# Off-diagonal and state's part of a scan step first, diagonal part behind them, sums of squares with 64 columns of ones

## The chip, the cores and the metric

The kernel runs on one core of a Trainium2 chip. The core has five engines that run on their own and wait for one another by semaphores: TensorE (matmuls; PE in the profile, PEld for the loads of its stationary operand), VectorE (DVE), ScalarE (ACT), GpSimd (POOL) and SyncE (SP), which here issues transfers. The time of a run is the device time of the core in microseconds (us). Lower is better. Each engine works through its own instructions in the order in which the program wrote them.

## The reference

Two layers on an input of 1024 tokens by 1024 features, float32. The first is a chunked spatial-gating MLP, the second a Mamba-2 mixer, then a final RMSNorm. The change lies in the second layer's scan, which has 8 groups of 4 heads (64 features a head, 128 states) and 8 chunks of 128 tokens:

```
cb    = einsum('bclgn,bcsgn->bclsg', Cm, Bm)
w_ls  = cb[..., None] * decay * dt
y_diag = einsum('bclsgj,bcsgjp->bclgjp', w_ls, x)
states = einsum('bclgn,bclgj,bclgjp->bcgjpn', Bm, decay_to_end * dt, x)
prev   = scan over chunks: carry * chunk_decay + states
y_off  = einsum('bclgn,bcgjpn,bclgj->bclgjp', Cm, prev, exp(dA_cs))
y      = y_diag + y_off + x * d_skip
gated  = rmsnorm over each group's 256 features of (y * silu(z))
h      = h + gated @ w_out
```

## The kernel before, in words

The first 1010 us hold the first layer and most of the second layer's input projection. Then comes the scan, in an order written out by hand: `scans()` walks over n = 0 to 63, with group g = n // 8 and chunk c = n % 8. Between the scan's own small matmuls TensorE is given full-size matmuls, so that it has work while the other engines prepare the next step. Up to n = 50 these are the rest of the input projection (tile `ab`, helper `mm3`, L134 to L136), behind it the first product of the output projection (tile `bo`, the same lines).

Step n does, in this order of the program:

- `pe_b(n)` on TensorE: the **diagonal part**, four matmuls, one for each head, which each give 64 of the 128 rows of tile `yy` (L1626: 64 columns of the array, so heads 0 and 2 go to the lower, 1 and 3 to the upper half); for c > 0 the **off-diagonal part**, two full-width matmuls whose stationary operand is the state after chunk c - 1 (L1630); for c < 7 the **state's part**, one full-width matmul with 256 moving columns into tile `sp` (L1637). At c = 3 and c = 7 `pe_b` gets a group as `ends` and adds that group's **sums of squares** (`sum_b`, L1702): squares `gsq`, summed over the partitions by a matmul with ones as stationary operand, two matmuls for two halves of 256 tokens, into rows 0 and 64 of the right half of `sp`. For the last group they are four, as the squares' two halves are not added up before. ScalarE copies rows 0 and 64 out (L1706).
- some projection matmuls; `pe_a(n + 2)`: three transposes and a matmul into tile `tp` (L1593, L1594).
- `weights(n + 1)` on VectorE: the weights `wl` of the next diagonal part (L1617), behind ScalarE's `decay` (L1599, L1601).
- `update(n)` on VectorE: the state after chunk c, from `sp` and the carried state (L1656; L1654 at c = 0). It stands directly behind `weights(n + 1)`.
- `out(n)`: VectorE reads `yy`, the off-diagonal half first (L1668), then the diagonal half twice (L1671).
- `drain()`: a step of the convolution on a finished projection tile (L1322 on VectorE, L1328 on ScalarE); its last one frees the tile `ab`.
- `tokens(n + 2)`: VectorE (L1607, L1609), ScalarE (L1611) and GpSimd (L1612) make the operands of step n + 2 from `tp`; `gate(n)` on GpSimd; at some steps squares, stores and loads; more projection matmuls.

Diagonal and off-diagonal parts write the two halves of one PSUM tile `yy`; `yy`, `sp` and `tp` rotate through four buffers. After the scan the output projection runs alone, with one more `sum_b` (tile `pr`, four matmuls) inside it.

Every fp32 matmul of L1593 to L1702 appears in the profile as two instructions (four heads are 8 rows x8, two sums x4), each with its own weight load.

Of the kernel before, what the change touches and what calls it, by code (L numbers as in the profile page):

```python
# [15 lines left out]
P = 128  # L16
# [13 lines left out]
def kernel(  # L30
# [21 lines left out]
    nc = tc.nc  # L52
    x = x[0]
    out = out[0]
# [42 lines left out]
    def sm(name):  # L97
        return ps[0].tile([P, 512], F32, name=name, tag="sm", bufs=n_sm[0])
# [65 lines left out]
    ones = cst.tile([P, P], F32, name="ones")  # L164
# [1399 lines left out]
    class Scan:  # L1564
# [55 lines left out]
        def pe_b(self, c, ends=None):  # L1620

            w, wl = self.cw[c], self.wl.pop(c)
            yy = sm("yy")
            for j in range(4):
                pt, f = j // 2, j % 2
                nc.tensor.matmul(out=yy[f * 64:(f + 1) * 64, pt * P:(pt + 1) * P], lhsT=w[:, j * 64:(j + 1) * 64],  # L1626
                                 rhs=wl[:, j, :], start=True, stop=True)
            if c > 0:
                for pt in range(2):
                    nc.tensor.matmul(out=yy[:, 256 + pt * P:384 + pt * P],  # L1630
                                     lhsT=self.state[c - 1][:, pt * P:(pt + 1) * P], rhs=self.x(3, c),
                                     start=True, stop=True)
            sp = None
            if c < 7 or ends is not None:
                sp = sm("sp")
            if c < 7:
                nc.tensor.matmul(out=sp[:, 0:256], lhsT=w[:, 512:640], rhs=w[:, 256:512], start=True, stop=True)  # L1637
            if ends is not None:
                ends.sum_b(sp[:, 256:512], 2 if ends.g == G - 1 else 1)
            self.ps[c] = yy, sp  # L1640
# [57 lines left out]
        def sum_b(self, pr=None, n=1):  # L1698
            pr = sm("pr") if pr is None else pr
            for m in range(n):  # L1700
                for h in range(2):
                    nc.tensor.matmul(out=pr[h * 64:h * 64 + 1, 0:256], lhsT=ones[:, 0:1],  # L1702
                                     rhs=self.sq[:, m, h * 256:(h + 1) * 256], start=m == 0, stop=m == n - 1)
            self.sr = self.sq[:, 1, 0:256]
            for h in range(2):
                nc.scalar.copy(out=self.sr[h * 64:h * 64 + 1], in_=pr[h * 64:h * 64 + 1, 0:256])  # L1706
# [314 lines left out]
```

## Time and profile before

| what | value |
|---|---|
| median of the 3 runs shown | 1517.45 us (1517.34 to 1518.26) |
| the profiled execution | 1520.45 us, its span 1518.6 us |
| TensorE matmuls | 1475.8 us busy (97%), 7834 instructions |
| VectorE | 1052.2 us (69%) |
| ScalarE | 783.3 us (52%) |
| GpSimd | 402.8 us (27%) |
| DMA | 254.45 MB, mean 168 GB/s |
| scan, from the first diagonal matmul to the last | 1021.7 to 1356 us |

A row of the view in order of time gives the start in us from the span's start, the time from the first start to the last end of what was merged in it, the engine, the line, the operation, the tiles (out<-in), the shapes, and in brackets the idle time ahead and what ended it. Ends of matmuls are modelled, and one matmul begins before the one ahead has ended, so that starts are compared with starts. "issue" is idle time for which the profile names no other engine. A busy share of 97% does not say that TensorE streams all that time: a matmul that lasts longer because its weights were not there counts as busy.

### The profile page before, as it was taken

To read this page: it belongs to the slowest core of one execution; us is meant where nothing else is said; L and a number is where in the kernel's file an instruction comes from. 1 tells how busy PE (TensorE), PEld (TensorE's weight loads), DVE (VectorE), ACT (ScalarE), POOL (GpSimd) and SP (SyncE) were. 2 spreads that over 40 slices of the span, in tenths; PEclk is the share of its full clock that TensorE was granted. 3 is DMA by queue.
4 is the path that set the end of the run, shared out by engine and by line. 5 is a ranking of instruction groups with operands and counts; after the bars stand their busy time and mean duration, and the time that the engine had idled before them with its cause. 6 is when DMAs were issued, how large, how long until landed. Compare 5 with 4: busy or idle time off the path is not lost. (4 is left out here: it accounts for less than half of the span.)

```text
span 1518.6 us, 21307 instructions
## 1 busy us (share of the span) xinstructions
PE 1475.8 (97%) x7834; PEld 1219.9 (80%) x7834; DVE 1052.2 (69%) x1713; ACT 783.3 (52%) x1256; POOL 402.8 (27%) x451
## 2 busy tenths in 40 slices
PE   6899999999999999999999999989999999999997
PEld 6899988888888888877878788877777777777875
DVE  7956566676666655678656467867677777688876
ACT  6433332322322445556566556656676666756463
POOL 1111110000000023202131323117677666643121
PEclk9999999999999999999999999999999999999999
DMA  5554323332322999947377978787656564679973
GB/s 183 140 173 140 105 89 111 108 107 98 116 86 79 357 255 241 250 140 159 104 178 159 189 162 165 149 231 203 187 165 170 160 191 137 171 248 277 257 149 111
DMA packets 174952, 254.45 MB, mean 168 GB/s; under 512 B 16400, under 2 KB 103168, under 8 KB 171648
## 3 DMA queue, kind: packets, MB, share of 16 engines
q1 hardware_dynamic: 124768, 168.93, 36.6%
q0 software_dynamic: 42448, 70.27, 23.0%
q10 hardware_dynamic: 7632, 13.90, 2.6%
q8 instruction: 62, 1.02, 0.3%
q14 instruction: 42, 0.34, 0.1%
HBM read 186.14 MB, written 51.18 MB: 156 GB/s over the span
## 5 line engine op out<-in xcount | busy, mean ns | idle before, releaser
L134 PE MATMUL acc<-hh,wh 128*128 128x512 f32 x868 | 339.9, 392 | 1.7 <-ACT u L296 1.4
L136 PE MATMUL acc<-hh,wl 128*128 128x512 f32 x868 | 338.5, 390 | 2.0 <-DVE wl L112 1.8
L135 PE MATMUL acc<-hl,wh 128*128 128x512 f32 x868 | 337.8, 389 | 0.0
L112 DVE TENSOR_TENSOR wl<-wr,wh 128x1024 fp32r<-128x1024 f32 (+1 forms) x96 | 114.3, 1192 | 119.4 <-ACT wh L111 119.3
L136 PEld LDWEIGHTS acc<-hh,wl 128*128 128x128 f32 x868 | 162.9, 188 | 37.8 <-DVE wl L112 3.7
L134 PEld LDWEIGHTS acc<-hh,wh 128*128 128x128 f32 x868 | 163.1, 188 | 36.1 <-ACT u L296 2.3
L135 PEld LDWEIGHTS acc<-hl,wh 128*128 128x128 f32 x868 | 163.0, 188 | 33.1
L296 ACT COPY u<-acc 128x512 f32<-128x512 f32 x115 | 66.9, 583 | 197.7 <-PE acc L136 197.6
L111 ACT CAST wh<-wr 128x1024 fp32r<-128x1024 f32 (+1 forms) x112 | 115.2, 1029 | 95.4 <-PE acc L135 56.7
L136 PE MATMUL acc<-wh,hl 128*128 128x256 f32 x448 | 128.6, 287 | 4.8 <-DVE hl L407 3.4
L134 PE MATMUL acc<-wh,hh 128*128 128x256 f32 x448 | 129.2, 288 | 3.0 <-ACT hh L398 1.1
L134 PE MATMUL ab<-hh,wh 128*128 128x512 f32 x288 | 128.2, 445 | 2.8 <-DVE zt L999 1.7
L135 PE MATMUL acc<-wl,hh 128*128 128x256 f32 x448 | 128.1, 286 | 1.1 <-DVE wl L421 1.1
L136 PE MATMUL ab<-hh,wl 128*128 128x512 f32 x288 | 113.4, 394 | 0.0
L135 PE MATMUL ab<-hl,wh 128*128 128x512 f32 x288 | 112.5, 390 | 0.1
L136 PEld LDWEIGHTS acc<-wh,hl 128*128 128x128 f32 x448 | 87.1, 194 | 5.9 <-DVE hl L407 4.1
L134 PEld LDWEIGHTS acc<-wh,hh 128*128 128x128 f32 x448 | 87.3, 195 | 3.9 <-ACT hh L398 1.3
L135 PEld LDWEIGHTS acc<-wl,hh 128*128 128x128 f32 x448 | 87.2, 195 | 1.6 <-DVE wl L421 1.4
L1599 ACT ACTIVATE wl<-wl,tk 128x128 f32<-128x128 f32 x256 | 81.6, 391 | 2.2 <-DMA wl<-cs_d 1.9
L649 POOL DMA_DIRECT2D y_d<-y x8 | 4.4, 549 | 291.3 <-DVE y L646 291.3
L135 PE MATMUL bo<-wl,xh 128*128 128x512 f32 x192 | 76.2, 397 | 3.5 <-DVE wl L742 1.8
L112 DVE TENSOR_TENSOR wl<-t,wh 128x1024 fp32r<-128x1024 f32 (+1 forms) x38 | 45.5, 1196 | 48.5 <-ACT wh L111 48.4
(317 smaller groups left out, 3255.1 us busy)
## 6 DMA issues: line engine op xcount, KB each, us to landing
wr<-in_a_w_in_dram SPq DMA_DIRECT2D x48, 512.0 KB, 3.7
wl<-cs_d SPq DMA_DIRECT2D x64, 256.0 KB, 3.4
wr<-in_b_w_in_dram SPq DMA_DIRECT2D x30, 512.0 KB, 9.1
wb<-in_a_w_out_dram SPq DMA_DIRECT2D x10, 1024.0 KB, 11.8
wb<-in_b_w_out_dram SPq DMA_DIRECT2D x10, 1024.0 KB, 11.1
wr<-in_b_w_in_dram SPq DMA_DIRECT2D x36, 256.0 KB, 8.0
v<-v_d SPq DMA_DIRECT2D x8, 1024.0 KB, 4.8
y_d<-y POOLq DMA_DIRECT2D x8, 1024.0 KB, 5.8
```

Source lines behind the costliest of these rows:

```text
L111: nc.scalar.copy(out=hi, in_=src)
L112: return (eng or nc.vector).tensor_tensor(out=lo, in0=src, in1=hi.bitcast(F32), op=ALU.subtract)
L134: nc.tensor.matmul(out=o, lhsT=l[0], rhs=r[0], start=start, stop=False, **kw)
L135: nc.tensor.matmul(out=o, lhsT=l[0], rhs=r[1], start=False, stop=False, **kw)
L136: nc.tensor.matmul(out=o, lhsT=l[1], rhs=r[0], start=False, stop=stop, **kw)
L296: nc.scalar.copy(out=self.u[n][:, i], in_=a)
L649: store = lambda: nc.gpsimd.dma_start(out=y_d[-1], in_=y)
L1599: nc.scalar.activation(wl[:, j, :], wl[:, j, :], AF.Relu, scale=-1.0, bias=tokc(2, c, self.g)[:, j:j + 1])
```

## The change

In `pe_b` the four diagonal matmuls move from the front to behind the state's part; the sums of squares stay last. In `sum_b` the stationary operand is 64 columns of ones instead of one, so that each sum is written to 64 rows of PSUM in place of one; ScalarE still reads one row of each half. Nothing else differs: the instructions of VectorE, ScalarE, GpSimd and SyncE stand in the same order with the same operands.

```
@@ pe_b
             w, wl = self.cw[c], self.wl.pop(c)
             yy = sm("yy")
-            for j in range(4):
-                pt, f = j // 2, j % 2
-                nc.tensor.matmul(out=yy[f * 64:(f + 1) * 64, pt * P:(pt + 1) * P], lhsT=w[:, j * 64:(j + 1) * 64],
-                                 rhs=wl[:, j, :], start=True, stop=True)
             if c > 0:
                 for pt in range(2):
                     nc.tensor.matmul(out=yy[:, 256 + pt * P:384 + pt * P],
...
             if c < 7:
                 nc.tensor.matmul(out=sp[:, 0:256], lhsT=w[:, 512:640], rhs=w[:, 256:512], start=True, stop=True)
+            for j in range(4):
+                pt, f = j // 2, j % 2
+                nc.tensor.matmul(out=yy[f * 64:(f + 1) * 64, pt * P:(pt + 1) * P], lhsT=w[:, j * 64:(j + 1) * 64],
+                                 rhs=wl[:, j, :], start=True, stop=True)
             if ends is not None:
                 ends.sum_b(sp[:, 256:512], 2 if ends.g == G - 1 else 1)
             self.ps[c] = yy, sp
@@ sum_b
-                    nc.tensor.matmul(out=pr[h * 64:h * 64 + 1, 0:256], lhsT=ones[:, 0:1],
+                    nc.tensor.matmul(out=pr[h * 64:h * 64 + 64, 0:256], lhsT=ones[:, 0:64],
                                      rhs=self.sq[:, m, h * 256:(h + 1) * 256], start=m == 0, stop=m == n - 1)
```

On TensorE, at the step n = 11 (c = 3 of the second group), the rows around `pe_b`, those of before with a minus and those of the change with a plus (`yy<-wl,cw` is the diagonal part, `yy<-xbc,state` the off-diagonal, `sp<-cw` the state's part, `sp<-gsq,ones` the sums):

```order
 L135 MATMUL ab<-hl,wh 128x512
 L136 MATMUL ab<-hh,wl 128x512
-L1626 MATMUL yy<-wl,cw 64x128 x4
-L1630 MATMUL yy<-xbc,state 128x128 x2
-L1637 MATMUL sp<-cw 128x256
-L1702 MATMUL sp<-gsq,ones 1x256 x2
+L1626 MATMUL yy<-xbc,state 128x128 x2
+L1633 MATMUL sp<-cw 128x256
+L1636 MATMUL yy<-wl,cw 64x128 x4
+L1702 MATMUL sp<-gsq,ones 64x256 x2
 L134 MATMUL ab<-hh,wh 128x512
 L135 MATMUL ab<-hl,wh 128x512
```

The diagonal's four matmuls, 64 rows of output each, now stand next to the sums, which have 64 rows too; the two full-width parts stand next to the projection.

On TensorE, at the first step, n = 0, which has no off-diagonal part:

```order
 L1593 MATMUL tp<-ident,xbc 128x128 x3
 L1594 MATMUL tp<-xbc 128x128
-L1626 MATMUL yy<-wl,cw 64x128 x4
-L1637 MATMUL sp<-cw 128x256
+L1633 MATMUL sp<-cw 128x256
+L1636 MATMUL yy<-wl,cw 64x128 x4
 L134 MATMUL ab<-hh,wh 128x512
 L135 MATMUL ab<-hl,wh 128x512
```

The state's part, which needs the operands of `tokens`, has changed places with the diagonal part, which needs `wl`.

On VectorE nothing moves; the rows of one step that the prediction speaks of (c = 2 of the second group, `t` is what L1668 makes of the off-diagonal half) stand so before and with the change:

```order
L1617 TENSOR_TENSOR wl<-wl,cw 128x512
L1656 TENSOR_TENSOR state<-sp,state 128x256
L1668 TENSOR_TENSOR t_8700<-yy,ze 128x256
L1671 SCALAR_TENSOR_TENSOR cw<-xbc,dsk,yy 128x128 x2
L1322 SCALAR_TENSOR_TENSOR bc<-ab,par,bc 128x1021
```

The weights of the next diagonal part are made directly ahead of the state that the next off-diagonal part loads.

More of the change, by code (lines that the diff above doesn't have):

```diff
@@ L1623, in pe_b @@
             yy = sm("yy")
[L1624 to L1627, printed above, removed]
             if c > 0:
@@ L1637, in pe_b @@
                 nc.tensor.matmul(out=sp[:, 0:256], lhsT=w[:, 512:640], rhs=w[:, 256:512], start=True, stop=True)
+            for j in range(4):
+                pt, f = j // 2, j % 2
+                nc.tensor.matmul(out=yy[f * 64:(f + 1) * 64, pt * P:(pt + 1) * P], lhsT=w[:, j * 64:(j + 1) * 64],
+                                 rhs=wl[:, j, :], start=True, stop=True)
             if ends is not None:
@@ L1701, in sum_b @@
                 for h in range(2):
-                    nc.tensor.matmul(out=pr[h * 64:h * 64 + 1, 0:256], lhsT=ones[:, 0:1],
+                    nc.tensor.matmul(out=pr[h * 64:h * 64 + 64, 0:256], lhsT=ones[:, 0:64],
                                      rhs=self.sq[:, m, h * 256:(h + 1) * 256], start=m == 0, stop=m == n - 1)
```

## The prediction

> **What bounds the kernel now.** I read the page's head first, then the waits of TensorE from 1010 us on, then the order in time of TensorE in two single steps of the scan, and last the places where TensorE stands still. The head:
>
> ```profile
> span 1518.6 us, 21307 instructions
> ...
> PE 1475.8 (97%) x7834; PEld 1219.9 (80%) x7834; DVE 1052.2 (69%) x1713; ACT 783.3 (52%) x1256; POOL 402.8 (27%) x451
> ```
>
> TensorE is the bound nearly everywhere, and VectorE (DVE), the next, has a third of its time free. The 64 steps of the scan, which are all that the diff touches, start between 1020.7 and 1355.2 us, with projection matmuls between them. In the waits of the weight loads (columns: who waited for what; us in all, times, longest) no data is named for most of the idle time before the scan's own matmuls:
>
> ```profile
> PEld yy L1626 <- issue: 15.0, 42, 0.4
> PEld yy L1630 <- issue: 7.7, 45, 0.2
> ```
>
> That is some 0.35 us ahead of each diagonal part and 0.17 us behind it, where the profile knows of no semaphore. What it is shows in the order in time (start, us, engine, line). A step without sums of squares, n = 25:
>
> ```profile
> 1155.29 0.39 PE L136 MATMUL ab<-hh,wl 128*128 128x512 f32 x1
> 1155.61 0.66 PE L1626 MATMUL yy<-wl,cw 128*64 128x128 f32 x8
> 1156.20 0.71 PE L1630 MATMUL yy<-xbc,state 128*128 128x128 f32 x4
> 1156.74 0.60 PE L1637 MATMUL sp<-cw 128*128 128x256 f32 x2
> 1156.99 0.58 PE L134 MATMUL ab<-hh,wh 128*128 128x512 f32 x1
> 1157.41 0.39 PE L135 MATMUL ab<-hl,wh 128*128 128x512 f32 x1
> ```
>
> And n = 27, with them (the last of these rows is of the weight loads):
>
> ```profile
> 1165.26 0.39 PE L136 MATMUL ab<-hh,wl 128*128 128x512 f32 x1
> 1165.58 0.66 PE L1626 MATMUL yy<-wl,cw 128*64 128x128 f32 x8
> 1166.16 0.71 PE L1630 MATMUL yy<-xbc,state 128*128 128x128 f32 x4
> 1166.71 0.60 PE L1637 MATMUL sp<-cw 128*128 128x256 f32 x2
> 1167.24 0.60 PE L1702 MATMUL sp<-gsq,ones 128*1 128x256 f32 x4
> 1167.77 0.50 PE L134 MATMUL ab<-hh,wh 128*128 128x512 f32 x1
> 1168.10 0.39 PE L135 MATMUL ab<-hl,wh 128*128 128x512 f32 x1
> 1165.57 0.42 PEld L1626 LDWEIGHTS yy<-wl,cw 128*64 128x64 f32 x8 [0.35 <-ACT wl L1601]
> ```
>
> The durations of single instructions (ns, min/median/max) come from the lines' own rows:
>
> ```profile
> L1626 PEld LDWEIGHTS yy<-wl,cw x512: 132/137/137, 1021.7 to 1355.9; 128*64 128x64 f32 x171
> L1630 PE MATMUL yy<-xbc,state x112: 275/275/377, 1026.9 to 1277.1; 128*128 128x128 f32 x112
> L1702 PEld LDWEIGHTS sp<-gsq,ones x64: 79/82/84, 1058.8 to 1357.3; 128*1 128x1 f32 x64
> L1702 PE MATMUL sp<-gsq,ones x64: 377/377/379, 1058.8 to 1357.5; 128*1 128x256 f32 x64
> ```
>
> Matmuls overlap, so I count from start to start. A projection matmul takes 0.23 us (L134 and L135 end at 1157.57 and 1157.80; the rest of its 0.39 overlaps the next). The two of sp last 0.60 together, and one of 256 columns 0.38 alone (L1702), so 256 columns stream in 0.22 us. The diagonal's eight run in pairs side by side (64 columns of the array each): 0.66 less 0.27 over three and a half steps, 0.11 us a pair, 0.44 in all. The off-diagonal's four take 0.11 each, 0.44.
>
> From 1155.29 to 1157.41 are 2.12 us. The two projection matmuls account for 0.46, the parts for 0.44 + 0.44 + 0.43; 0.35 are left over, which is one way into the narrow tile and back: the diagonal starts 0.09 after the stream ahead has ended (1155.61 against 1155.29 + 0.23), 0.05 of its first load lies bare, and at its end 0.10 pass before the full-width load, whose first matmul takes 377 instead of 275 ns. With the sums of squares the same stretch is 1168.10 - 1165.26 = 2.84 us, 0.72 more. Their four matmuls are two pairs, 0.43 to 0.44 us; **0.29 us is a second way in and back**, from 128 columns to one and out again.
>
> **The change part by part.** *Order alone.* Off-diagonal and sp now join the projection matmuls at full width without a break, then one way in, diagonal, one way out into the projection. It is still one way in and back per step, of the same pieces: the exit into a projection matmul is measured behind the sums of squares, where L134 lasts 0.50 instead of 0.39 us. So 0 for the 49 steps without sums, between -0.01 and +0.02 us each, hence -0.5 to +1 in all.
>
> *64 columns of ones, behind the diagonal.* In the 15 steps with sums (c = 7 of every group, c = 3 of all but the first) diagonal and sums now have the same tile shape, and one of the two ways in and back goes: 0.29 us a step at most, 15 x 0.29 = 4.4 us. No row shows a 64-column matmul behind another with other data, but the diagonal's pairs, which change halves at every instruction without a gap, are near. The Trainium skill (TensorEngine Tiling (Array Packing), Key Properties) says that changing the tiling mode, not merely the tile, drains the engine, which is this reading; no run so far shows it for these sums.
>
> The wider load lasts 137 instead of 82 ns. The eight loads of the diagonal together span 0.42 us beside matmuls that begin at the same instant, so I cost it at nothing: a 0.22 us stream covers it. Uncovered it is 0.055 x 72 instructions = 4.0 us. The eight instructions at 1369 us (four `pr` sums inside the last projection) gain nothing.
>
> *What is waited for first.* Before, the step's first wait was for wl (L1617); now it is for the state (L1656), which VectorE makes right behind wl, and so always later. What that costs is read where it is late (DVE rows, then TensorE):
>
> ```profile
> 1090.48 0.69 DVE L1617 TENSOR_TENSOR wl<-wl,cw 128x512 f32<-128x512 f32 x1 [1.29 <-ACT wl L1601]
> 1091.09 0.42 DVE L1656 TENSOR_TENSOR state<-sp,state 128x256 f32<-128x256 f32 x1
> 1090.45 0.40 PE L136 MATMUL ab<-hh,wl 128*128 128x512 f32 x1
> 1091.27 0.66 PE L1626 MATMUL yy<-wl,cw 128*64 128x128 f32 x8 [0.42 <-issue]
> 1165.15 0.41 DVE L1656 TENSOR_TENSOR state<-sp,state 128x256 f32<-128x256 f32 x1
> 1157.45 0.43 DVE L1656 TENSOR_TENSOR state<-sp,state 128x256 f32<-128x256 f32 x1 [2.57 <-PE sp L1637]
> ```
>
> At n = 13 the diagonal waited 0.50 us (1091.27, due at 1090.45 + 0.32). The state is done at 1091.51; with 0.10 to the load (as from wl's end, 1091.17, to 1091.27) and 0.10 of bare load, the off-diagonal begins at 1091.71, 1.03 after TensorE is free at 1090.68. VectorE itself waited for ScalarE there, so nothing brings it forward: **+0.53 us**. At n = 27 the state is done at 1165.56, TensorE free at 1165.49: 0.27 us lost, which eats that step's 0.29. In the usual step it is done at 1157.88 and wanted 2.6 us later (steps are some 5 us apart); 0.
>
> Behind an off-diagonal that waits stand, on TensorE, sp, diagonal and projection, in that order; for sp VectorE's next state waits, and so the next step.
>
> *sp earlier.* Its end moves from 2.05 us after the step's last projection matmul (1156.74 + 0.60 - 1155.29) to 0.23 + 0.44 + 0.43 + 0.16 (what 377 ns has beyond its stream) = 1.27, 0.78 earlier. The diagonal ends at 1.86, in time for the instruction that reads it, two behind the state's. VectorE is ahead by 0.78 wherever it stood waiting for sp. Mostly that buys nothing. Once it does:
>
> ```profile
> 1271.99 0.42 DVE L1656 TENSOR_TENSOR state<-sp,state 128x256 f32<-128x256 f32 x1 [2.46 <-PE sp L1637]
> 1273.18 1.27 DVE L1322 SCALAR_TENSOR_TENSOR x<-ab,par,x 128x1021 f32<-128x1021 f32 x1
> 1274.50 0.50 PE L134 MATMUL ab<-hh,wh 128*128 128x512 f32 x1 [0.68 <-DVE x L1322]
> ```
>
> From the wait for sp VectorE runs through to the end of L1322, which frees the projection's accumulator; TensorE stands 0.85 us before it (the 0.68 shown and the 0.16 by which matmuls else overlap). 0.78 of that goes: **-0.77 us**; bounds 0 and -0.85.
>
> *First step.* There sp comes first, and waits for ScalarE's copy instead of wl:
>
> ```profile
> 1020.99 0.27 ACT L1611 COPY cw<-tp 128x128 f32<-128x128 f32 x1
> 1020.71 0.95 DVE L1617 TENSOR_TENSOR wl<-wl,cw 128x512 f32<-128x512 f32 x1
> ```
>
> The copy ends at 1021.26, wl at 1021.66; sp's 0.43 us fit between and the way into the diagonal follows: -0.2 us (0 to -0.4).
>
> *Where a saving is swallowed.* Two places do not belong to TensorE (chain of waits):
>
> ```profile
> 1295.45 1.23 POOL gsq L1696
> 1296.73 0.60 PE sp L1702 x4
> ...
> 1337.23 0.55 PE sp L1702 x4
> ...
> 1379.79 0.50 PE bo L135
> ```
>
> At n = 51 the sums wait for GpSimd, whose chain goes back to VectorE's wait at 1271.99: that chain moves by the 0.77 above, and what n = 47 and n = 51 save is waited away. From the sums of n = 59 at 1337.23 the chain runs over ScalarE and VectorE to 1379.79, so that n = 63 saves nothing, and its later state costs nothing either; n = 59 itself counts. Behind 1380 us all moves along.
>
> **Sum:** 15 steps less n = 27, 47, 51 and 63 are 11 x 0.29 = 3.2; + 0.77 + 0.2 - 0.53 = 3.6 us. The profiled execution took 1520.45 us (1.85 around the span), to be 1516.8; the median of the runs shown, 1517.45, is 3.0 below it, and I take the same 3.6 off: **1513.9 us**.
>
> **Rivals.** *Swallowed further.* TensorE reaches each step sooner, so states with little to spare come late, as at n = 27. Half the 3.2 lost and the 0.77 not gained: 1.6 + 0.2 - 0.5 = 1.3 us, 1516.2. For it: VectorE's stand at 1271.99 is the only such relief I found. Against: most chains start at TensorE and move with it.
>
> *The sums still drain behind the diagonal* (the change does not do what it says): 0 instead of 3.2, so 0.4 us saved, 1517.0. Against it, the pairs without a gap.
>
> *Wider loads in the open:* 1513.9 + 4.0 = 1517.9. Against it, the 0.42 us for eight loads. The Trainium skill (TensorE: Matmul & The Clock Gate, Part 3, The mechanism) has weight loads overlap running matmuls only where the row groups differ; all these use the same 128 rows, so by that rule the loads would lie bare; the trace disagrees.
>
> *Slower:* the state's load, now the first of the step, is not brought ahead under the projection's last matmul, in all 56 steps that have one. The price per step is n = 27's, 0.27 us, 15 us in all: 1529. It decides from 3.6 / 56 = 0.06 us a step, and is slower by over 0.2% from 0.12. For it, n = 13 and 27. Against it, 2.6 us to spare in the usual step, and full-width loads that now overlap all along.
>
> **Numbers.** A measurement of this kernel tells about 0.2% (3 us) from no change, so 1514.4 is the border. Forecast 0.60; swallowed 0.22; still draining 0.08; loads bare 0.03; slower 0.07. Faster 0.60, same 0.33, slower 0.07. Low end: all 15 steps, 0.85 and 0.4 gained, nothing lost, is 5.6 us, 1511.8. High end 1517.2, past the swallowed case and the draining one.
>
> **What would show it.** Right: in a step with sums the stretch from the last projection matmul to the second behind falls from 2.84 to 2.55 us, with no gap between L1636 and L1702, and without sums it stays 2.12; the stall at 1274.5 is gone and that at n = 13 is about 1.0 us. Wrong: a gap of 0.09 before L1702 (still draining), L1702 matmuls more than 0.22 apart (bare loads), or waits before L1626 in more than a handful of steps (the state).

## The result, and the profile after

The changed kernel takes 1514.16 us, the median of 18 runs (1512.83 to 1517.23); the kernel before takes 1517.39 us beside it (18 runs). The ratio is 0.9979, with a 95% interval of 0.9972 to 0.9985, so 3.2 us are gained, between 2.3 and 4.2. The gain is clear of zero; whether it passes the border of 1514.4 us that the prediction set isn't decided, since that lies inside the interval (0.9980). The profiled execution took 1512.85 us, its span 1511.1. From the head of its page:

```profile
PE 1471.6 (97%) x7834; PEld 1222.5 (81%) x7834; DVE 1053.7 (70%) x1713; ACT 783.3 (52%) x1256; POOL 401.5 (27%) x451
```

The matmuls are as many as before. A step with sums of squares, n = 35, in the order in time of TensorE (start, us, engine, line):

```profile
1204.67 0.39 PE L136 MATMUL ab<-hh,wl 128*128 128x512 f32 x1
1204.90 0.60 PE L1626 MATMUL yy<-bc,state 128*128 128x128 f32 x4
1205.34 0.60 PE L1633 MATMUL sp<-cw 128*128 128x256 f32 x2
1205.87 0.66 PE L1636 MATMUL yy<-wl,cw 128*64 128x128 f32 x8
1206.36 0.60 PE L1702 MATMUL sp<-gsq,ones 128*64 128x256 f32 x4
1206.89 0.50 PE L134 MATMUL ab<-hh,wh 128*128 128x512 f32 x1
1207.22 0.39 PE L135 MATMUL ab<-hl,wh 128*128 128x512 f32 x1
```

From 1204.67 to 1207.22 are 2.55 us; before, the same stretch took 2.84. The off-diagonal follows the projection after 0.23 us, which is that matmul's stream alone. The sums (1206.36) follow the diagonal (1205.87) after 0.49: 0.44 for its four pairs and the 0.05 of its own bare first load, and no gap. A step without sums, n = 25, stays at 2.12 us:

```profile
1151.04 0.39 PE L136 MATMUL ab<-hh,wl 128*128 128x512 f32 x1
...
1153.16 0.40 PE L135 MATMUL ab<-hl,wh 128*128 128x512 f32 x1
```

The places where TensorE stood still read differently now. At n = 13, where it waits for the state (the last answer of each line is who released it):

```profile
1086.49 0.40 PE L136 MATMUL ab<-hh,wl 128*128 128x512 f32 x1
1087.69 0.68 PE L1626 MATMUL yy<-xbc,state 128*128 128x128 f32 x4 [0.80 <-DVE state L1656]
...
1089.66 0.39 PE L135 MATMUL ab<-hl,wh 128*128 128x512 f32 x1
```

The off-diagonal starts 1.20 after the projection matmul instead of 0.23, so the stall is 0.97, and the stretch 3.17 us. Before the projection matmul of n = 46 it waits 0.24 us instead of 0.85:

```profile
1267.76 0.39 PE L1594 MATMUL tp<-bc 128*128 128x128 f32 x2
1268.22 0.50 PE L134 MATMUL ab<-hh,wh 128*128 128x512 f32 x1
```

The two matmuls of L1594 stream 0.11 each, to 1267.98. The waits of TensorE between 1010 and 1360 us (who waited for what; us in all, times, longest) have a new head:

```profile
PE yy L1626 <- DVE state L1656: 1.5, 3, 0.8
```

These are n = 13, 51 and 63. Before, no such row stood there.

How far the gain reaches is seen by cutting the span at two steps (us from the step's last projection matmul, worked out from the order in time of each trace):

| profiled execution | n = 1 to n = 59 | n = 59 to the end | span |
|---|---|---|---|
| before | 309.24 | 183.46 | 1518.6 |
| after | 306.65 | 182.22 | 1511.1 |
| after, profiled again | 306.59 | 182.21 | 1513.9 |

So the change is worth 2.6 us between n = 1 and n = 59, and the 0.3 of n = 59 itself behind. What else lies between the two spans is not the change. About 3.7 us come ahead of n = 1, which starts between 1022.2 and 1025.9 us in the executions profiled, with either order: 0.8 of them in the step n = 0, of which more below, 1.0 at a stand for VectorE (L999), which lasts 0.7 to 1.7 us from profile to profile in work that the diff doesn't touch, and the rest further ahead. And in the tail the profiled execution of before had some microseconds at a lower granted clock. Stretches by window (us, busy time of each engine, then the granted clock), before, then after:

```profile
1380.00:1385.00 5.00, 5.00 (x16) 3.96 (x16) 5.00 (x7) 4.64 (x4) 0.49 (x1) 0.66 0.97 211
```

```profile
1380.00:1385.00 5.00, 5.00 (x23) 4.13 (x23) 4.19 (x6) 3.07 (x4) 2.65 (x3) 1.00 1.08 254
```

16 matmuls were started there in the one and 23 in the other. A run of the old order that kept the full clock there (64 columns alone, below) takes 182.63 us from n = 59 to the end, only 0.4 more than the changed kernel. That is why the two spans differ by 7.5 us and the medians by 3.2: single spans are not compared here, stretches between two steps are.

### The profile page after: what moved, and what is told of

The parts are those of the page before. It is cut to its first block, busy times and chain, and to the rows that moved or that the text cites. A ratio compares the mean times of both kernels' runs of the same rounds, so it can differ in the third digit from the quotient of the medians.

```text
span 1511.1 us, 21297 instructions
## 1 busy us (share of the span) xinstructions
PE 1471.6 (97%) x7834; PEld 1222.5 (81%) x7834; DVE 1053.7 (70%) x1713; ACT 783.3 (52%) x1256; POOL 401.5 (27%) x451
## 5 line engine op out<-in xcount | busy, mean ns | idle before, releaser
L134 PE MATMUL ab<-hh,wh 128*128 128x512 f32 x288 | 124.7, 433 | 1.2 <-DVE zt L999 0.7
```

Of the source, the lines that this page charges most:

```text
L134: nc.tensor.matmul(out=o, lhsT=l[0], rhs=r[0], start=start, stop=False, **kw)
```

## The experiments

All stretches below are, as above, from the start of a step's last projection matmul to the start of the second projection matmul behind it. The ratios are to the kernel before, run beside each. Except for three runs (64 columns alone, the diagonal cut in two, `sp` last) their intervals meet that of the changed kernel (0.9972 to 0.9985), so that the times of whole runs don't tell them from it, and the conclusions rest on the stretches.

### The order alone, with one column of ones

```
-   nc.tensor.matmul(out=pr[h * 64:h * 64 + 64, 0:256], lhsT=ones[:, 0:64],
+   nc.tensor.matmul(out=pr[h * 64:h * 64 + 1, 0:256], lhsT=ones[:, 0:1],
```

(against the changed kernel)

> The changed order with one column of ones, as before the change. Theory (every change of the tile's shape on TensorE costs about 0.09 us of waiting and a bare first load; the sums have to have the diagonal's shape to be free of it): 0.09 to 0.15 us between the diagonal and the sums, so a step with sums takes 2.65 to 2.70 us from the last projection matmul to the second behind it, not 2.55, and the time is 1.0 to 1.7 us above the change (11 or 12 steps that count). Rival 1 (the order alone brings it, anything narrow behind something narrow runs on): no gap, the time of the change. Rival 2 (the sums pay a whole way in and back, 0.29 us): 2.84 us a step, 3.2 us above the change.

Measured: 1516.37 us (11 runs, 1514.94 to 1517.12), ratio 0.9988 (0.9976 to 0.9999). n = 35:

```profile
1208.30 0.40 PE L136 MATMUL ab<-hh,wl 128*128 128x512 f32 x1
...
1209.50 0.66 PE L1636 MATMUL yy<-wl,cw 128*64 128x128 f32 x8
1210.09 0.60 PE L1702 MATMUL sp<-gsq,ones 128*1 128x256 f32 x4
...
1210.96 0.39 PE L135 MATMUL ab<-hl,wh 128*128 128x512 f32 x1
```

The sums start 0.59 behind the diagonal instead of 0.49: with one column there is a gap of 0.10. The stretch is 2.66 us, so it lies between the 2.84 of before and the 2.55 of after. **The order alone saves 0.19 of the 0.29 us**, and the 64 columns the other 0.10.

### 64 columns alone, in the old order

```
-   nc.tensor.matmul(out=pr[h * 64:h * 64 + 1, 0:256], lhsT=ones[:, 0:1],
+   nc.tensor.matmul(out=pr[h * 64:h * 64 + 64, 0:256], lhsT=ones[:, 0:64],
```

(against the kernel before)

> The order of before with 64 columns of ones. Theory: diagonal and sums stand apart, with full-width matmuls between them, so both ways in and back stay; the first load of the sums lies 0.05 us barer: 2.84 to 2.90 us in a step with sums, 0 to 0.8 us above the kernel before. Rival (64 columns are by themselves the cheaper form): a step with sums falls below 2.75 us, and the time lies 1.5 to 3 us below the kernel before.

Measured: 1517.58 us (11 runs, 1515.93 to 1519.38), ratio 1.0001 (0.9992 to 1.001). n = 35:

```profile
1206.54 0.39 PE L136 MATMUL ab<-hh,wl 128*128 128x512 f32 x1
...
1208.52 0.65 PE L1702 MATMUL sp<-gsq,ones 128*64 128x256 f32 x4
...
1209.44 0.39 PE L135 MATMUL ab<-hl,wh 128*128 128x512 f32 x1
```

The stretch is 2.90, 0.05 more than before: L1702 lasts 0.65 instead of 0.60, because the first of its loads, which stands behind a change of shape, lies bare, and is 137 instead of 82 ns long. The three others are hidden; bare, all four would have cost 0.22. So the wider load costs something only at the first place behind a change of shape, and in the changed kernel the sums don't stand there.

### 32 columns in the new order

```
-   nc.tensor.matmul(out=pr[h * 64:h * 64 + 64, 0:256], lhsT=ones[:, 0:64],
+   nc.tensor.matmul(out=pr[h * 64:h * 64 + 32, 0:256], lhsT=ones[:, 0:32],
```

> The change with 32 columns of ones in place of 64. Theory (the tile's shape decides, and 32 columns are another shape than 64): the gap between diagonal and sums of the run with one column, 0.09 to 0.15 us, and its time, 1.0 to 1.7 us above the change. Rival (what counts is that more than one column is loaded, or that the sums stand behind the diagonal): no gap, the time of the change.

Measured: 1515.09 us (11 runs, 1513.89 to 1519.61), ratio 0.9988 (0.9979 to 0.9997). n = 35:

```profile
1207.96 0.66 PE L1636 MATMUL yy<-wl,cw 128*64 128x128 f32 x8
1208.55 0.63 PE L1702 MATMUL sp<-gsq,ones 128*32 128x256 f32 x4
```

Again 0.59 from the diagonal to the sums, the gap of 0.10 that one column shows, and a first load 0.03 barer; the stretch is 2.68. What counts is the same shape as the neighbour's, not a narrow one. The Trainium skill (TensorEngine Tiling (Array Packing), Key Properties) says that the engine drains when the tiling mode changes and not when only the tile does. The trace agrees: from 64 to 64 columns 0, from 64 to 32 or to one 0.10 us.

### The sums in front of the diagonal

```
     sp
+    sums of squares
     diagonal
-    sums of squares
```

> The change with the sums ahead of the diagonal part instead of behind it, still next to it and of its shape. Theory (only that the two stand side by side counts): the same 2.55 us in a step with sums, no gap between them, the time within 1 us of the change. Rival (the sums run on without a gap only where they follow): a gap of about 0.1 us, 1 to 2 us above the change.

Measured: 1515.25 us (12 runs, 1512.91 to 1517.18), ratio 0.9979 (0.9967 to 0.9991). n = 35:

```profile
1206.52 0.39 PE L136 MATMUL ab<-hh,wl 128*128 128x512 f32 x1
...
1207.71 0.65 PE L1702 MATMUL sp<-gsq,ones 128*64 128x256 f32 x4
1208.20 0.61 PE L1638 MATMUL yy<-wl,cw 128*64 128x128 f32 x8
...
1209.07 0.39 PE L135 MATMUL ab<-hl,wh 128*128 128x512 f32 x1
```

2.55 us, as after, and from the sums to the diagonal 0.49: the sums' 0.43 and the bare first load, which is now theirs. For the changes of shape it doesn't matter on which side of the diagonal the sums stand, so long as nothing of another width lies between. It does for the squares: the sums want them 0.5 us sooner, and wait for GpSimd at n = 15 and n = 51, whose stretches are 0.25 and 0.43 us longer than in the changed kernel.

### The diagonal cut in two

Two of its four matmuls stand in front of the off-diagonal, and two behind `sp`, so each step has a second way in and back.

```
+    for j in (0, 1): diagonal
     off-diagonal
     sp
-    for j in range(4): diagonal
+    for j in (2, 3): diagonal
```

> The change with two of the four diagonal matmuls put back in front of the off-diagonal part, the other two left behind the state's part: nothing more is computed, but in all 64 steps TensorE goes into the narrow tile and back once more. Theory (one way in and back costs 0.35 us wherever it stands): a step without sums goes from 2.12 to 2.47 us, and the time lies some 20 us above the change (59 steps ahead of the stretch that other engines set, 59 x 0.35), 1534. Rival 1 (the cost belongs to the neighbourhood of the projection's matmuls, and between the scan's own parts it is less): 2.2 to 2.3 us a step, 6 to 12 us above the change. Rival 2 (the idle times shown as issue are other engines' work and move elsewhere): within 3 us of the change.

Measured: 1532.39 us (3 runs, 1532.32 to 1533.17), ratio 1.0096 (1.007 to 1.0122), 18.2 us above the changed kernel. A step without sums, n = 26:

```profile
1160.54 0.39 PE L136 MATMUL ab<-hh,wl 128*128 128x512 f32 x1
1160.86 0.44 PE L1626 MATMUL yy<-wl,cw 128*64 128x128 f32 x4
...
1162.31 0.44 PE L1640 MATMUL yy<-wl,cw 128*64 128x128 f32 x4
...
1163.02 0.40 PE L135 MATMUL ab<-hl,wh 128*128 128x512 f32 x1
```

2.48 us against 2.12, with the same matmuls. **A way in and back costs 0.35 us**, as the prediction had counted it out of what was left over in a step of before. Some 59 steps by 0.35 are 20.6 us; the waits for the state at n = 13, 27, 49, 51 and 63, which this order hides behind the first half of the diagonal, give a part of it back.

### `sp` last

```
     off-diagonal
-    sp
     diagonal
     sums of squares
+    sp
```

> The order off-diagonal, diagonal, sums with 64 columns, state's part last: the same number of ways in and back as in the change, but sp as late as before the change. Theory (the sums save 0.29 us a step whatever stands behind; sp earlier is worth only the stand of TensorE at 1274 us before the change, 0.6 to 0.8 us): steps with sums 2.55 us, the stand in front of the projection at the end of n = 46 back to 0.7 to 0.9 us from 0.24, the time 0 to 1.2 us above the change. Rival (sp earlier carries a good part of the gain, by VectorE and GpSimd being ahead everywhere): stands of TensorE in several more places, 2 us or more above the change.

Measured: 1524.36 us (7 runs, 1521.68 to 1528.82), ratio 1.0047 (1.0028 to 1.0067). It was meant to take away the earlier end of `sp` alone. The wait before n = 46's projection matmul does come back, to the same 0.68 as before:

```profile
1281.15 0.50 PE L134 MATMUL ab<-hh,wh 128*128 128x512 f32 x1 [0.68 <-DVE x L1322]
```

So the gain there came from `sp`'s earlier end. But the edit brought a wait of its own, which decides its time. The waits of TensorE, and n = 19, with ScalarE's copy:

```profile
PE sp L1639 <- ACT gsq L1706: 9.5, 7, 2.9
```

```profile
1125.68 1.22 PE L1639 MATMUL sp<-cw 128*128 128x256 f32 x2 [2.88 <-ACT gsq L1706]
1124.89 0.73 ACT L1706 COPY gsq<-sp 1x256 f32<-1x256 f32 x2
```

State's part and sums share one tile in PSUM, one in the left half and one in the right. With the sums first, the state's matmul waits until ScalarE has copied the sums out (1124.89 + 0.73), though it writes the other half. It happens in the seven steps with c = 3 that have both. In the changed kernel the state's half is written first, and the copy stands in nobody's way. As a test of the 0.78 us that `sp` ends earlier it is spoilt by this, and its time says nothing of it beyond the row at n = 46.

### The state ahead of the weights on VectorE

What the change had made worse are steps in which the off-diagonal waits for a state that VectorE makes right behind the next weights. The remedy that this suggests is to turn the two round:

```
+            at("update", n)
             if n > 0:
                 at("weights", n + 1)
-            at("update", n)
```

> The change, and on VectorE the state's update ahead of the next weights instead of behind them. Theory (what the change lost, it lost where the off-diagonal part, now first, waits for a state that VectorE makes behind the weights): the waits before L1626 at n = 13 (0.97 us), 27 (0.23), 49 (0.25) and most of that at 51 (0.46) go, the diagonal behind has its weights in time, and the time is 1 to 2 us below the change. Rival (the update in front waits for sp and holds the weights up, so the wait only moves to the diagonal part): waits of 0.3 us or more before the diagonal part in several steps, the time within 0.5 us of the change or above it.

Measured: 1513.60 us (10 runs, 1512.04 to 1515.58), ratio 0.9975 (0.9966 to 0.9984). Run again beside the changed kernel:

> The run with the update ahead of the weights once more, beside the change. Theory (the waits for the state at n = 13, 27 and 49 are gone, but 0.37 us at n = 15 and 0.33 us at n = 51 are given back to GpSimd's sum of the squares, and what n = 63 saves is waited away by the chain that begins at n = 59): 0.6 to 0.9 us below the change. Rival (nothing is left of it): within 0.3 us.

> The changed kernel unaltered, beside the next two on the same chip. Theory and rivals alike: 0.9979 of the kernel before, within the interval 0.9972 to 0.9985.

1513.59 us (10 runs), 0.9971 (0.9961 to 0.998), against 1515.13 us (11 runs), 0.9984 (0.9975 to 0.9992). n = 13, VectorE and then TensorE:

```profile
1085.17 0.42 DVE L1656 TENSOR_TENSOR state<-sp,state 128x256 f32<-128x256 f32 x1
1086.56 0.69 DVE L1617 TENSOR_TENSOR wl<-wl,cw 128x512 f32<-128x512 f32 x1 [0.96 <-ACT wl L1601]
1086.57 0.39 PE L136 MATMUL ab<-hh,wl 128*128 128x512 f32 x1
1086.80 0.61 PE L1626 MATMUL yy<-xbc,state 128*128 128x128 f32 x4
```

The state is ready (1085.59) 1.2 us before TensorE is free (1086.80), and the diagonal behind it still finds its weights. The waits at n = 13, 27, 49 and 63 are gone: their stretches fall by 1.05, 0.31, 0.33 and 0.60. Two others, n = 15 and n = 51, grow, both for the squares from GpSimd, and the one before n = 46's projection matmul comes partly back (the waits of TensorE between 1010 and 1360):

```profile
PE sp L1702 <- POOL gsq L1696: 0.9, 2, 0.7
PE ab L134 <- DVE x L1322: 0.9, 2, 0.5
```

Of some 1.7 us taken away ahead of n = 59, 0.6 to 0.7 arrive there, less than the 1 to 2 us first expected (305.98 and 305.96 us from n = 1 to n = 59, against 306.65 and 306.59). And the 0.60 taken away at n = 63 leave the stretch from n = 59 to the end as it was: 182.70 and 182.21, against 182.22 and 182.21. That end isn't TensorE's, as the prediction said. By whole runs the swap isn't shown to be faster than the changed kernel beside it: the two intervals meet.

### The swap, and the squares added on VectorE

```
-            nc.gpsimd.tensor_tensor(out=self.sq[:, 0, :], in0=self.sq[:, 0, :], in1=self.sq[:, 1, :], op=ALU.add)
+            nc.vector.tensor_tensor(out=self.sq[:, 0, :], in0=self.sq[:, 0, :], in1=self.sq[:, 1, :], op=ALU.add)
```

(with the swap above)

> The run with the update ahead of the weights, and the addition of the two halves of the squares (L1696, 1.3 us on GpSimd) on VectorE. Theory (behind the state the next thing waited for is that addition): the waits of the sums at n = 15 and n = 51 go, 0.4 and about 1.1 us in the order in time, and the time is 1 to 2 us below the run without this. Rival (GpSimd's other work, the carry of the state above all, is what n = 51 waits for, or VectorE is late in turn): the waits stay or move, the time within 0.5 us of it.

Measured: 1513.15 us (7 runs, 1511.83 to 1514.34), ratio 0.997 (0.9959 to 0.9981). The sums wait for nobody any more; at n = 51 the wait has moved to the state, as the rival had it. VectorE is early there, and stands 1.20 us for GpSimd's share of the state (L1647):

```profile
1289.91 0.42 DVE L1656 TENSOR_TENSOR state<-sp,state 128x256 f32<-128x256 f32 x1 [1.20 <-POOL state L1647]
1290.48 0.68 PE L1626 MATMUL yy<-bc,state 128*128 128x128 f32 x4 [0.65 <-DVE state L1656]
```

305.27 us from n = 1 to n = 59, 0.7 less than with the swap alone, where 1 to 2 us were expected. It has the lowest time of all, but the runs don't tell it from the swap (0.9971), and its interval meets that of the changed kernel run beside it (0.9984); better than the changed kernel is likely, and not shown.

## Why the prediction was right

The forecast was 1513.9 us and the time is 1514.16. Its sum was 3.6 us; the traces give 2.9 (2.6 up to n = 59 and 0.3 of that step), and the medians 3.2 with an interval that holds both. That the time lies only 0.3 us from the forecast is partly luck: three of the terms below were too kind by 0.16 to 0.2 us, all in the same direction, and the profiles differ by more than that at places that the change doesn't touch. The measured terms below add up to 3.1; the rest is hundredths in the many steps without sums, and waits for transfers. By its terms:

| term | predicted, us | measured, us |
|---|---|---|
| 11 steps with sums | -3.2 | -3.2 (0.29 each, 0.28 to 0.31) |
| steps without sums, order alone | 0 (-0.5 to +1) | -0.01 to 0.01 each |
| n = 13, the state late | +0.53 | +0.54 |
| n = 27, its 0.29 eaten | 0 | +0.01 |
| n = 47 to 51, swallowed | 0 | about +0.17 |
| stall at n = 46 | -0.77 | -0.61 |
| first step | -0.2 | 0, or -0.16 where TensorE stands there |
| n = 63 | 0 | 0 at the end |

**Right: one way in and back less.** The sum's largest term came from counting out a step of before, row by row. Both the size (0.29) and the steps that keep it came out, and the step without sums stayed at 2.12 us. The diagonal cut in two confirms the 0.35 from the other side.

**Right: the state late at n = 13 and n = 27.** Reading when VectorE had the state ready before, and adding the 0.10 to the load and the 0.10 bare, gave 1.03 us of stall, and 0.97 were measured. The swap on VectorE shows that it is the order of weights and state there that causes it, since both waits vanish with it.

**Mis-sized: "0.78 of that goes".** The prediction took VectorE ahead by the whole 0.78 us by which `sp` ends earlier, and said that the diagonal ends "in time for the instruction that reads it, two behind the state's". The instruction in between was overlooked. VectorE at n = 46 (L1668 reads only the off-diagonal half), after, with TensorE's diagonal:

```profile
1265.33 0.66 PE L1636 MATMUL yy<-wl,cw 128*64 128x128 f32 x8
1265.51 0.42 DVE L1656 TENSOR_TENSOR state<-sp,state 128x256 f32<-128x256 f32 x1 [2.23 <-PE sp L1633]
1266.04 0.42 DVE L1668 TENSOR_TENSOR t<-yy,ze 128x256 f32<-128x256 f32 x1
1266.89 1.28 DVE L1322 SCALAR_TENSOR_TENSOR x<-ab,par,x 128x1021 f32<-128x1021 f32 x1
```

Before, L1668 started 0.34 behind L1656; now it is 0.53, at 1266.04, right behind the diagonal's end at 1265.99. It waits for the matmul that wrote `yy` last, which is now the diagonal, though it reads only the other half. The trace has it wait there for TensorE's semaphore, which it didn't before, and in 27 of the 56 steps with an off-diagonal it starts 0.05 us behind the diagonal's end. These 0.19 us are the difference between 0.77 and 0.58 to 0.61.

**Mis-sized: "what n = 47 and n = 51 save is waited away".** Both savings were counted as nothing, and that was too kind by 0.17 us. n = 47 saves its 0.29, but TensorE reaches n = 49 earlier than the state is there, which costs 0.33. At n = 51 two waits stand in one step:

```profile
1288.64 0.68 PE L1626 MATMUL yy<-bc,state 128*128 128x128 f32 x4 [0.30 <-DVE state L1656]
1290.58 0.65 PE L1702 MATMUL sp<-gsq,ones 128*64 128x256 f32 x4 [0.23 <-POOL gsq L1696]
1288.07 0.42 DVE L1656 TENSOR_TENSOR state<-sp,state 128x256 f32<-128x256 f32 x1 [1.21 <-POOL state L1647]
```

Both go back to GpSimd: VectorE made that state late because it had stood 1.21 us for GpSimd's share of it. That step is 0.13 longer than before. The rival "swallowed further" had named this mechanism and priced it at half the sums' gain; it is there in two steps only.

**Not the change's: "-0.2 us" at the first step.** The profiled executions of before and after differ by 0.81 us at n = 0. But with the old order and 64 columns there is no stall either (1.56 us, as after). Whether it comes depends on whether TensorE or the weights and copies are ready first there, which changes from profile to profile; what decides that isn't shown. It isn't the stand at some 995 us: that was 1.64 us in a profile without the stall and 1.20 in one with it. Where it came in the new order, in the changed kernel's second profile, the wait was indeed for ScalarE's copy:

```profile
1020.67 0.67 PE L1633 MATMUL sp<-cw 128*128 128x256 f32 x2 [0.36 <-ACT cw L1611]
1022.19 0.39 PE L135 MATMUL ab<-hl,wh 128*128 128x512 f32 x1
1019.98 0.95 DVE L1617 TENSOR_TENSOR wl<-wl,cw 128x512 f32<-128x512 f32 x1
```

From the end of the weights (1020.93) to the second projection matmul are 1.26 us; before, from 1021.66 to 1023.08, 1.42. So the step gains 0.16 when it stands and nothing when it doesn't, and it stood in two of eight profiles with the new order and in one of two with the old. As a term of the sum it was a reading of one execution.

**Wrong, though it moved no number: what each part of the change does.** The prediction gave all of the 0.29 to the 64 columns, and made the rival "the sums still drain behind the diagonal" cost the whole 3.2 us. One column behind the diagonal does drain, as that rival has it, and still 0.19 of the 0.29 is saved. A step's changes of shape are not equally dear. Counted out of the rows:

| change of shape | us |
|---|---|
| full width to 64 columns | 0.09 to 0.10 wait, 0.05 of the first load bare |
| 64 columns to full width | 0.10 wait, 0.10 of the first load bare |
| full width to one column | 0.10 |
| 64 columns to 32 or one | 0.10, and 0.03 bare with 32 |
| 64 columns to 64 | 0 |

With the matmuls' streams at 2.20 us in a step with sums, before has 0.14 + 0.20 + 0.10 + 0.20 more, 2.84. The order alone takes away one way out, 0.20. The 64 columns take away the 0.10 between two narrow shapes. The rival, had it held, would by these rows have been some 1.1 us above the measured time (11 steps by 0.10), not 3.2.

**The slower rival**, a state's load not brought ahead under the last projection matmul in all 56 steps, didn't come: off-diagonals follow the projection after 0.23 us, which leaves no room for a bare load, in all steps but those where the state itself is late.

What stays open: between n = 10 and 11 and between n = 42 and 43 the two profiles differ by +0.30 and -0.42 us, at waits for transfers that also come and go between two profiles of the same kernel. What causes them isn't shown.

## What to carry to other kernels

Count a matmul sequence by its changes of shape as well as by its matmuls: what the profile calls issue ahead of a load was here the price of a change, and it can be summed from start to start. Put parts of the same width side by side, widen a small part to its neighbour's width where its load is covered, and keep everything else at full width in one piece. Then look for what the new first part waits for, and for readers and writers that share a tile in PSUM: here both waited for the other half of the tile, too.

## What the runs showed of the hardware that was not expected

**The way out is dearer than the way in**, 0.20 against 0.14 us, mostly because the full-width load behind it, 190 ns long, lies more open than one of 64 columns, 137 ns: 0.10 us against 0.05, with 0.02 to 0.03 for 32 columns (109 ns) and nothing for one (82 ns), so that in each case some 80 to 90 ns of the load are hidden. Loads of 1, 32, 64 and 128 columns lasted 82, 109, 137 and 190 ns: some 0.85 ns a column and some 80 ns besides. The Trainium skill (TensorE: Matmul & The Clock Gate, LDWEIGHTS (loading the stationary operand)) has a load's time as the columns over 1.2 GHz, which is 0.83 ns a column, about this slope, and none of the 80 ns.

**Loads overlap matmuls on the same rows.** With no change of shape, the sums' loads of 64 columns cost nothing behind the diagonal, although all use the same 128 rows. The Trainium skill (TensorE: Matmul & The Clock Gate, Part 3, The mechanism) has them overlap only where the row groups differ, and the trace disagrees; what the same section says ahead of it, that a load may also be pulled ahead into a background weight buffer, fits.

**A stall of TensorE can cost twice.** Behind the 3 us at n = 19 with `sp` last, matmuls of full width started 0.43 us apart instead of 0.23, for six microseconds. By window, the granted clock is the third number from the end:

```profile
1122.80:1125.68 2.88, 0.00 (x1) 0.00 (x1) 1.47 (x4) 2.81 (x7) 1.29 (x2) 0.85 0.28 92
1125.68:1130.00 4.32, 4.32 (x12) 3.45 (x13) 2.46 (x5) 1.88 (x5) 1.30 (x2) 0.50 0.02 4
1130.00:1135.00 5.00, 5.00 (x28) 4.05 (x28) 2.31 (x6) 2.94 (x7) 3.33 (x3) 0.84 0.05 11
```

The stalls of up to 1 us in the changed kernel show no such thing. Behind 1010 us the kernel before had it in the profile once, at 1380 us, behind a stall of 1.78 us; the other eleven profiles have a stall of 1.70 to 1.80 us at the same place and full clock behind it. Why it came in that one is not shown.
